# Half of a turned tile's small transfers issued on another queue, with new step tables, in a two-layer encoder trunk

## Chip, cores and metric

The kernel runs on one core of a Trainium2 chip. The metric is the device time of one execution in microseconds (us), less is better. A NeuronCore has five engines with an instruction queue each: TensorE (PE, matrix products), VectorE (DVE), ScalarE (ACT), GpSimd (POOL) and SyncE (SP, which here only issues transfers). Transfers are also issued by POOL. Whichever engine issues them, they run on the core's 16 DMA engines.

## The reference

The input x is 256 tokens by 2048 features, float32. Layer 1 is forgetting attention and a squared-ReLU MLP; layer 2 is chunked attention with a relative bias against keys and values that are projected once, and a second MLP:

```python
u = rms_norm(h, a_norm_g)
q, k, v, fz = split(u @ a_w_in)                # 16 heads of 128
h = h + forgetting_attention(...) @ a_w_out
h = h + square(relu(rms_norm(h, g) @ w1)) @ w2   # 2048 -> 8192 -> 2048
k_sh, v_sh = split(rms_norm(h, kv_norm_g) @ kv_w)
q = rms_norm(rms_norm(h, b_norm_g) @ b_w_q)
h = h + chunked_relbias_attention(q, k_sh, v_sh, b_rel) @ b_w_out
h = h + square(relu(rms_norm(h, g) @ w1)) @ w2
```

All weights are float32, about 497 MB, and each is read once from HBM.

## The kernel before

**Products.** A weight block of 128 rows and 1024 columns is loaded (`raw`), split by ACT into a rounded part `hi` (line 294) and by DVE into the rest `lo` (line 295), and multiplied in three passes, x-high by hi, x-low by hi, x-high by lo (lines 594, 596, 598). The two MLPs and layer 2's query projection save products by a Strassen-like scheme. Their weights come in pairs of blocks; for each pair seven forms (`FORMS`: "11", "T3", "T2", "T1", "21", "T4", "22") are multiplied with sums of the activations (`form_products`, line 618), and the rest of the pair's rows in plain steps "a" and "b". Some forms are sums of weight blocks: `bring` (line 309) loads a block with SP into a tile `w`, `add_on` (line 316) adds another block onto it, for T1 and T3 by an accumulating transfer that POOL issues (line 326), for T4 by DVE (line 324), and `make` (line 328) forms T2 with DVE (line 333).

**Turned tiles.** The result of a product has tokens on the partitions, but the next product needs features there. A tile of 128 partitions by 1024 elements is turned in two parts. DVE transposes its 32x32 blocks into `z` (`blocks32`, line 440, instruction on line 443); then 16 small transfers move the 32-row blocks of z to their places in `q` or `land` (`moves`, line 452, transfers on line 458). Each has 32 rows of 256 elements, 32 KB. `moves` returns four steps, of four transfers each. It is used for the new x after an output projection or an MLP (`next_x`, line 492), for the hidden activations (`turn_hidden`, line 975) and for two of layer 2's query tiles (`head_norm` with `apart`). What reads the turned tile is, for x, ACT's scaling `y` (line 419, in `split_turned`), and, for the hidden activations, ACT's ReLU in place (line 956, in `take`). Tiles elsewhere are turned through DRAM (`carry`), which the change leaves alone.

**Order.** The program text is the order of DVE, ACT, PE and SP (`keep_order`); POOL's instructions have their order from the framework that places them. Each engine works through its own queue in order. A list of fill slots runs beside the products: after each step of a plan one slot is taken off (`run_fill`, line 357), and its functions are written there. Which slot a step goes to, counted from where its tile became complete, is set by tables:

- `HIDDEN[n]`: for the n-th quarter of a hidden chunk, four move steps, then the steps of `take` (ReLU first).
- `SHORT[n]` and `LONG[n]`: for the n-th quarter of a new x after an output projection (SHORT) or an MLP's end (LONG): row sums, block transposes, four move steps, then the steps of `split_turned` (y first).
- `QUERY`, `ATT`: slots of query tiles and of the attention heads.
- `ORDER`: the steps of a pair; "f0" to "f6" are forms (two halves each), "a" and "b" plain steps, "r" a step left over from an earlier pair. An "r" is passed over when nothing is left (lines 217 to 219).
- `BEHIND[(i, s)]`: what is written some number of weight units after form i, half s, was issued: (delay, own pair or next, function, arguments).
- `OPENING`: the same ahead of a plan's first pair.

**Buffers and waits.** Weight units are issued up to three ahead of the product (`fetch`, line 348), and loaded up to four units ahead of that; `raw` has three buffers of two halves. A load that needs a buffer waits on SP until the split of the block before it is done, and what is written behind it on SP waits too.

Of the kernel before, what the change touches and what calls it, by code (L numbers as in the profile page):

```python
# [28 lines left out]
AHEAD = 2  # L29
EARLY = 4  # L30
HIDDEN = (
# [4 lines left out]
)  # L36
UA = UN // 512
LONG = (
# [4 lines left out]
)  # L43
SHORT = (
# [4 lines left out]
)  # L49
REL = 384  # L50
QUERY = (0, 1, 13, 12, 6, 17, 6)
AGAIN = (0, 1, 2, 3, 5, 5, 7, 7)
ATT = ((8, 14, 18, 18, 10), (8, 9, 12, 12, 9))
BIAS = (3, 6, 7)
ORDER = {
# [9 lines left out]
}  # L65
BEHIND = {
    (0, 0): [(0, 1, "make", 0), (4, 1, "add", "T1", 0)],
    (0, 1): [(0, 1, "make", 1)],
    (1, 1): [(3, 0, "bring", "12", 0), (3, 1, "add", "T1", 1)],
    (3, 1): [(5, 0, "bring", "11", 0), (3, 0, "bring", "11", 1)],  # L70
    (4, 0): [(0, 1, "add", "T4", 0)],
    (4, 1): [(0, 1, "add", "T4", 1), (9, 0, "add", "T3", 1)],
    (2, 1): [(3, 0, "bring", "12", 1)],
    (3, 0): [(2, 0, "add", "T3", 0)],
}
SUBS = {"1": (2, 2), "2": (2, 2), "q": (2, 2)}
OPENING = (
    (23, "bring", "12", 0),
    (17, "bring", "12", 1),
    (4, "add", "T3", 0),  # L80
    (9, "add", "T3", 1),
    (6, "bring", "11", 0),
    (1, "bring", "11", 1),
)
BIG = 2 * UN
FORMS = ("11", "T3", "T2", "T1", "21", "T4", "22")
# [14 lines left out]
def trunk(ctx: ExitStack, tc: tile.TileContext, t):  # L101
# [3 lines left out]
    V, S, G, TE, SY = nc.vector, nc.scalar, nc.gpsimd, nc.tensor, nc.sync  # L105
# [40 lines left out]
    first = sm.tile([P, GH], F32, name="first", bufs=1)  # L146
# [299 lines left out]
    def deal(at, do):  # L446
        items = [[] for _ in range(max(at) + 1)]
        for i, d in zip(at, do):
            items[i].append(d)
        add_fill(items)  # L450

    def moves(z, dst):
        n = z.shape[1] // 4
        d = dst.rearrange("p (i f) -> p i f", i=4)

        def move(i):
            for j in range(4):
                SY.dma_start(d[32 * j : 32 * j + 32, i], z[32 * i : 32 * i + 32, j * n : (j + 1) * n])  # L458

        return [lambda i=i: move(i) for i in range(4)]  # L460

# [19 lines left out]
    def landing(i):  # L481
        if not land:
            land.append(prob.tile([P, 2 * BIG], F32, name="land", tag="p", bufs=1))
        return land[0][:, i * UN : (i + 1) * UN]

    def turned(name=None):
        z = qkv.tile([P, GH * T], F32, name="z")
        return (z, qkv.tile([P, GH * T], F32, name=name, tag=name, bufs=4 if name == "s" else 2)) if name else z
# [186 lines left out]
    def head_norm(stats, z, dst, late=0, apart=None):  # L675

        rest = []

        def f(b, ps):
            sq = wk.tile([P, 512], F32, name="sq", tag="wk")  # L680
            ss = sm.tile([P, GH], F32, name="ss")
            rn = sm.tile([P, GH], F32, name="rn")

            def square():
                S.activation(sq, ps, AF.Square)

            def total():
                V.tensor_reduce(ss, sq.rearrange("p (a d) -> p a d", a=GH), axis=AX.X, op=ALU.add)

            def norm():  # L690
                vv = sm.tile([P, GH], F32, name="vv")
                V.tensor_scalar(vv, ss, 1.0 / P, stats().e[:, b : b + 1], op0=ALU.mult, op1=ALU.add)
                G.tensor_tensor(rn, vv, mhalf, op=ALU.pow)

            def turn():
                qn = wk.tile([P, 512], F32, name="qn", tag="wk")
                V.tensor_tensor(qn.rearrange("p (a d) -> p a d", a=GH), ps.rearrange("p (a d) -> p a d", a=GH),
                                rn.unsqueeze(2).to_broadcast([P, GH, P]), op=ALU.mult)
                blocks32(qn, z, b)

            if apart is None:
                square()
            rest.append((square, total, norm, turn))
            if b == NB - 1:
                turns = [[t] for _, _, _, t in rest]
                turns += carry(z, dst) if apart is None else [[m] for m in moves(z, dst)]
                if apart is not None:
                    add_fill([[]] * apart + [[s, t, n] for s, t, n, _ in rest] + turns)
                    return
                for _, total, norm, _ in rest:  # L710
                    total()
                    if not late:
                        norm()
                add_fill([[]] * (late - 1) + ([[n for _, _, n, _ in rest]] if late else []) + turns)
        return f

    def scale_q(land, layer, g):
        tag = "qs"[g // 2]
        q = qkv.tile([P, GH, T], F32, name="q", tag=tag, bufs=4 if tag == "s" else 2)
        S.activation(q.rearrange("p a (b i c) -> p (a b) i c", b=NB, i=4),  # L720
                     land.rearrange("p (i ab c) -> p ab i c", i=4, c=32), AF.Copy, scale=gqk[:, layer : layer + 1])
        return q
# [66 lines left out]
    def attend(g, q, k, v, cq, o, make_bias):  # L789
        st = [{} for _ in range(GH)]  # L790
        box = {}
        k4 = k.rearrange("p (i a b c) -> p a b i c", i=4, a=GH, b=NB)
        *at, far = ATT[g == NG - 1]
        items = [[] for _ in range(at[-1] + far + 1)]
# [16 lines left out]
    def add_fill(items):  # L811
        for i, it in enumerate(items):
            if i < len(fill):
                fill[i] = fill[i] + it
            else:
                fill.append(it)
# [210 lines left out]
    def query(g):  # L1027
        box = {}

        def f(b, ps):  # L1030
            if b == 0:
                z, lq = turned(), landing(2 + g % 2)
                box["lq"], box["f"] = lq, head_norm(lambda: st2, z, lq, apart=(*QUERY[:2], None, None)[g])
            box["f"](b, ps)
            if b == NB - 1:
                add_fill([[]] * QUERY[2 + g] + [[lambda: qs.append(scale_q(box["lq"], 1, g))]])
                if g == 1:
                    add_fill([[]] * QUERY[6] + [[st2.flip]])
                    deal(AGAIN, [again[i // 2] for i in range(8)])
# [105 lines left out]
```

## Time and profile before

| | us |
|---|---|
| median of 3 runs | 2152.24 |
| the runs | 2150.33, 2152.24, 2157.17 |
| the profiled execution's own time | 2150.54 |
| its span in the trace | 2148.8 |
| POOL busy | 168.5 |
| HBM | 239 GB/s over the span |

The profile comes from one execution. In its rows a line such as L458 is a line of the kernel; "x672" is the number of instructions, three numbers after it are the least, the middle and the largest duration in ns. A row of a timeline holds the start, the time up to the last end, the engine, the line and the operation; the square brackets behind it give how long the engine had been idle before, and what ended that. A row of the waits holds the waiting instruction, the one that released it, the total in us, the number of waits and the longest. SPq and POOLq are the queues of instructions that issue transfers or wait. "DMA q<-z" is a transfer from z to q in the chain that ended last, from its issue to its landing.

### The profile page before, as it was taken

How to read it: one execution, taken by the hardware profiler on the slowest of the kernel's cores; microseconds unless marked ns; L12 is line 12 of the kernel's file. 1: busy time of each engine (PE TensorE's matmuls, PEld its weight loads, DVE VectorE, ACT ScalarE, POOL GpSimd, SP SyncE). 2: the span in 40 equal slices, each digit the busy share in tenths (PEclk: the TensorE clock that was granted, in tenths of full speed). 3: DMA queues.
4: the chain of work that ended last, by engine and by line, in shares of the span. 5: the costliest groups of instructions: out<-in, count | busy, mean ns of one | idle time of the engine just before them, and what ended most of it. 6: DMA issues, size and time to landing. Idle time of an engine off the chain costs nothing.

```text
span 2148.8 us, 26598 instructions
## 1 busy us (share of the span) xinstructions
PE 2086.3 (97%) x9114; PEld 1697.6 (79%) x9114; DVE 1738.3 (81%) x2003; ACT 1305.8 (61%) x1567; POOL 168.5 (8%) x184
## 2 busy tenths in 40 slices
PE   9999998999999999999999999988999999999999
PEld 7888887787887887887777888877778878878877
DVE  6777775899889889888998577758898888898887
ACT  6544444667567567657676444456665675675574
POOL 1101000001001000000002000000010010000000
PEclk9999999999999999999999999999999999999999
DMA  8787786788888888889786877867788888888884
GB/s 297 238 253 234 243 249 221 246 252 257 270 265 250 254 275 252 269 260 288 223 255 201 260 230 229 266 207 247 240 261 278 263 239 259 278 253 266 265 282 156
DMA packets 166519, 538.86 MB, mean 251 GB/s; under 512 B 42848, under 2 KB 79856, under 8 KB 131568
## 3 DMA queue, kind: packets, MB, share of 16 engines
q1 hardware_dynamic: 146800, 465.86, 61.5%
q0 software_dynamic: 19584, 71.31, 18.8%
q8 instruction: 71, 1.16, 0.2%
q14 instruction: 64, 0.52, 0.1%
HBM read 497.20 MB, written 15.75 MB: 239 GB/s over the span
## 4 chain that ended last, share of the span: by engine, by line
PE 79%; DVE 8%; DMA 5%; issue 3%; SPq 3%; ACT 2%; ACTq 0%; DVEq 0%
PE acc L596 17%; PE acc L594 17%; PE acc L598 16%; PE po L598 5%; PE po L594 5%; PE po L596 5%; PE s L598 4%; PE s L594 4%; PE s L596 4%; DVE lo L295 4%; SPq L458 2%; ACT hi L294 2%; DMA q<-z 2%; DMA raw<-in_s2a 1%; DVE wT L324 1%
## 5 line engine op out<-in xcount | busy, mean ns | idle before, releaser
L295 DVE TENSOR_TENSOR lo<-raw,hi 128x1024 fp32r<-128x1024 f32 (+1 forms) x634 | 761.8, 1215 | 237.8 <-ACT hi L294 212.1
L294 ACT ACTIVATE hi<-raw 128x1024 fp32r<-128x1024 f32 (+1 forms) x634 | 661.8, 1054 | 418.8 <-PE acc L596 226.6
L594 PE MATMUL acc<-hi,act 128*128 128x512 f32 x1644 | 461.5, 396 | 23.3 <-ACT hi L294 14.5
L596 PE MATMUL acc<-hi,act 128*128 128x512 f32 x1644 | 451.4, 391 | 0.0
L598 PE MATMUL acc<-lo,act 128*128 128x512 f32 x1644 | 450.4, 390 | 0.8 <-DVE lo L295 0.8
L594 PEld LDWEIGHTS acc<-hi,act 128*128 128x128 f32 x1644 | 306.3, 188 | 94.1 <-ACT hi L294 18.1
L598 PEld LDWEIGHTS acc<-lo,act 128*128 128x128 f32 x1644 | 308.4, 188 | 68.6 <-DVE lo L295 3.8
L596 PEld LDWEIGHTS acc<-hi,act 128*128 128x128 f32 x1644 | 310.2, 189 | 66.2 <-DVE act L389 0.5
L294 ACT ACTIVATE hi<-w 128x1024 fp32r<-128x1024 f32 x204 | 214.9, 1056 | 95.0 <-PE acc L596 38.9
L295 DVE TENSOR_TENSOR lo<-w,hi 128x1024 fp32r<-128x1024 f32 x204 | 244.4, 1218 | 26.2 <-ACT hi L294 25.3
L295 DVE TENSOR_TENSOR lo<-wT,hi 128x1024 fp32r<-128x1024 f32 x136 | 163.0, 1220 | 21.7 <-ACT hi L294 21.5
L294 ACT ACTIVATE hi<-wT 128x1024 fp32r<-128x1024 f32 x136 | 142.3, 1057 | 59.8 <-PE acc L596 20.3
L594 PE MATMUL s<-hi,act 128*128 128x512 f32 x476 | 138.5, 396 | 11.4 <-ACT hi L294 11.2
L598 PE MATMUL s<-lo,act 128*128 128x512 f32 x476 | 138.0, 394 | 4.5 <-DVE lo L295 4.2
L596 PE MATMUL s<-hi,act 128*128 128x512 f32 x476 | 136.8, 392 | 0.2 <-DVE act L423 0.2
L594 PEld LDWEIGHTS s<-hi,act 128*128 128x128 f32 x476 | 89.6, 190 | 33.3 <-ACT hi L294 15.0
L598 PEld LDWEIGHTS s<-lo,act 128*128 128x128 f32 x476 | 87.8, 188 | 30.1 <-DVE lo L295 12.9
L596 PEld LDWEIGHTS s<-hi,act 128*128 128x128 f32 x476 | 90.4, 190 | 19.8 <-DVE act L423 0.6
L324 DVE TENSOR_TENSOR wT<-wT,raw 128x1024 f32<-128x1024 f32 x68 | 82.8, 1218 | 0.0
L333 DVE TENSOR_TENSOR wT<-w,w 128x1024 f32<-128x1024 f32 x68 | 82.8, 1218 | 0.0
L594 PE MATMUL po<-hi,act 128*128 128x512 f32 x272 | 72.8, 389 | 0.0
L596 PE MATMUL po<-hi,act 128*128 128x512 f32 x272 | 72.7, 389 | 0.0
(181 smaller groups left out, 2158.2 us busy)
## 6 DMA issues: line engine op xcount, KB each, us to landing
raw<-in_w_in SPq DMA_DIRECT2D x94, 512.0 KB, 5.9
raw<-in_s1a SPq DMA_DIRECT2D x32, 1024.0 KB, 6.5
raw<-in_s2a SPq DMA_DIRECT2D x32, 1024.0 KB, 7.3
raw<-in_w_kv SPq DMA_DIRECT2D x64, 512.0 KB, 5.7
raw<-in_s1b SPq DMA_DIRECT2D x32, 1024.0 KB, 6.0
raw<-in_s2b SPq DMA_DIRECT2D x32, 1024.0 KB, 7.0
q<-z SPq DMA_DIRECT2D x672, 32.0 KB, 4.5
raw<-in_w_oa SPq DMA_DIRECT2D x32, 512.0 KB, 5.7
```

Of the source, the lines that this page charges most:

```text
L294: S.activation(hi[:, c], raw[:, c], AF.Copy)
L295: V.tensor_tensor(lo[:, c], raw[:, c], hi[:, c].bitcast(F32), op=ALU.subtract)
L324: V.tensor_tensor(d, d, p.t["21", s], op=ALU.add)
L333: V.tensor_tensor(p.t["T2"][:, half(s)], p.t["T3"][:, half(s)], p.t["11"][:, half(s)], op=ALU.add)
L458: SY.dma_start(d[32 * j : 32 * j + 32, i], z[32 * i : 32 * i + 32, j * n : (j + 1) * n])
L594: TE.matmul(ps, xh, cut(hi, j), start=first, stop=False, **kw)
L596: TE.matmul(ps, xl, cut(hi, j), start=False, stop=False, **kw)
L598: TE.matmul(ps, xh, cut(lo, j), start=False, stop=last, **kw)
```

## The change

In `moves`, of the four transfers in a step the second and the fourth are issued by POOL (`G`), the first and third still by SP. Besides, the entries of the tables for slots, orders and delays are set anew. No other line differs.

```diff
--- before.py
+++ after.py
@@ -29,58 +29,56 @@
 AHEAD = 2
 EARLY = 4
 HIDDEN = (
-    (2, 2, 3, 3, 6, 8, 8, 9, 11, 11),
-    (0, 0, 2, 2, 7, 8, 8, 8, 10, 10),
-    (0, 1, 3, 3, 5, 5, 9, 9),
-    (1, 2, 2, 4, 6, 6, 9, 10),
+    (1, 3, 3, 3, 6, 8, 8, 9, 11, 11),
+    (0, 2, 2, 2, 7, 8, 8, 8, 10, 10),
+    (1, 1, 1, 5, 5, 5, 9, 9),
+    (1, 1, 3, 4, 4, 6, 8, 10),
 )
 UA = UN // 512
 LONG = (
-    (1, 0, 0, 0, 0, 1, 6, 6, 6, 9),
-    (1, 0, 0, 1, 2, 3, 6, 7, 7, 10),
-    (2, 0, 0, 0, 4, 6, 7, 7),
-    (0, 0, 1, 1, 4, 4, 8, 8),
+    (1, 0, 0, 0, 0, 0, 5, 5, 5, 5),
+    (1, 0, 0, 0, 3, 4, 6, 7, 7, 10),
+    (0, 0, 0, 0, 0, 5, 7, 7),
+    (0, 0, 1, 2, 4, 5, 8, 8),
 )
 SHORT = (
     (3, 0, 0, 0, 0, 0, 3, 3, 5, 5),
-    (8, 0, 0, 1, 2, 5, 6, 10, 14, 14),
-    (1, 0, 2, 2, 2, 3, 8, 10),
-    (0, 0, 1, 1, 1, 3, 5, 5),
+    (6, 0, 0, 1, 1, 5, 8, 9, 14, 14),
+    (0, 0, 2, 2, 3, 5, 8, 10),
+    (1, 0, 1, 1, 1, 3, 5, 5),
 )
 REL = 384
-QUERY = (0, 1, 13, 12, 6, 17, 6)
+QUERY = (0, 1, 15, 10, 5, 17, 5)
 AGAIN = (0, 1, 2, 3, 5, 5, 7, 7)
-ATT = ((8, 14, 18, 18, 10), (8, 9, 12, 12, 9))
+ATT = ((8, 14, 18, 18, 10), (8, 8, 12, 12, 9))
 BIAS = (3, 6, 7)
 ORDER = {
-    "first": "f0 r r f1 r r r f2 f3 a a r f4 f6 f5 a a b b",
-    "w10": "f0 f1 r f2 r r f4 f3 r f5 f6 a r a a a b b",
-    "w11": "f0 r f1 r f2 f4 a r f3 a a f5 a f6 b b",
-    "w20": "r f0 r r f1 f2 f4 f3 f5 a r r a b f6 b",
-    "w21": "f0 f1 f2 r f3 f4 r a f5 r r r a f6 b r",
+    "first": "f0 r r f1 r r r r f2 f3 a r a f4 r f6 f5 a a b b",
+    "w10": "f0 f1 r f2 r r f4 f3 r r f5 a f6 a a a b b",
+    "w11": "f0 r f1 r f2 f4 a r f3 r a a f5 a f6 b b",
+    "w20": "r f0 r r f1 f2 f4 f3 f5 a r r a r b f6 b",
+    "w21": "f0 f1 f2 r f3 f4 r a f5 r r f6 r b a r",
     "w20+": "r f0 r f1 f2 f4 f3 f5 a a b b f6",
-    "w21+": "f0 f1 r r f2 r r r f4 r r f5 f3 a a r f6 r a a b b",
+    "w21+": "f0 f1 r r f2 r r r r f4 r f5 f3 a a r f6 r a a b b",
     "q0": "f0 r f1 r r f2 f3 f4 a a f5 f6 b b",
-    "q1": "f0 f1 r f2 r f4 a f5 r r a r f3 b b f6",
+    "q1": "f0 f1 r f2 r f4 r a f5 r r f3 a b b f6",
 }
 BEHIND = {
-    (0, 0): [(0, 1, "make", 0), (4, 1, "add", "T1", 0)],
+    (0, 0): [(2, 1, "add", "T1", 0), (0, 1, "make", 0)],
     (0, 1): [(0, 1, "make", 1)],
-    (1, 1): [(3, 0, "bring", "12", 0), (3, 1, "add", "T1", 1)],
+    (1, 1): [(2, 0, "bring", "12", 0), (3, 1, "add", "T1", 1), (4, 0, "bring", "12", 1)],
     (3, 1): [(5, 0, "bring", "11", 0), (3, 0, "bring", "11", 1)],
-    (4, 0): [(0, 1, "add", "T4", 0)],
-    (4, 1): [(0, 1, "add", "T4", 1), (9, 0, "add", "T3", 1)],
-    (2, 1): [(3, 0, "bring", "12", 1)],
-    (3, 0): [(2, 0, "add", "T3", 0)],
+    (4, 0): [(0, 1, "add", "T4", 0), (1, 0, "add", "T3", 0)],
+    (4, 1): [(0, 1, "add", "T4", 1), (8, 0, "add", "T3", 1)],
 }
 SUBS = {"1": (2, 2), "2": (2, 2), "q": (2, 2)}
 OPENING = (
     (23, "bring", "12", 0),
-    (17, "bring", "12", 1),
-    (4, "add", "T3", 0),
+    (19, "bring", "12", 1),
+    (6, "add", "T3", 0),
     (9, "add", "T3", 1),
-    (6, "bring", "11", 0),
-    (1, "bring", "11", 1),
+    (3, "bring", "11", 0),
+    (4, "bring", "11", 1),
 )
 BIG = 2 * UN
 FORMS = ("11", "T3", "T2", "T1", "21", "T4", "22")
@@ -455,7 +453,7 @@
 
         def move(i):
             for j in range(4):
-                SY.dma_start(d[32 * j : 32 * j + 32, i], z[32 * i : 32 * i + 32, j * n : (j + 1) * n])
+                (SY, G)[j % 2].dma_start(d[32 * j : 32 * j + 32, i], z[32 * i : 32 * i + 32, j * n : (j + 1) * n])
 
         return [lambda i=i: move(i) for i in range(4)]
```

## The prediction

> **What bounds the kernel now.** The page comes first: what is busy, and what the chain that ended last is made of.
>
> ```profile
> span 2148.8 us, 26598 instructions
> ...
> PE 2086.3 (97%) x9114; PEld 1697.6 (79%) x9114; DVE 1738.3 (81%) x2003; ACT 1305.8 (61%) x1567; POOL 168.5 (8%) x184
> ...
> PE 79%; DVE 8%; DMA 5%; issue 3%; SPq 3%; ACT 2%; ACTq 0%; DVEq 0%
> ```
>
> TensorE is the bound. All its idle time is 2148.8 - 2086.3 = 62.5 us, with start and tail in it, so a change to the transfers can win some tens of us at most. POOL is nearly idle; an issuing instruction on SP isn't counted as busy, so SP has to be read elsewhere. The second view is the timeline of PE, for the waits that it shows in brackets.
>
> ```profile
> 356.25 1.21 PE L594 MATMUL acc<-hi,act 128*128 128x512 f32 x4 [2.28 <-ACT hi L294]
> 371.89 2.07 PE L594 MATMUL acc<-hi,act 128*128 128x512 f32 x4 [4.24 <-ACT hi L294]
> ...
> 423.20 2.08 PE L594 MATMUL s<-hi,act 128*128 128x512 f32 x4 [3.87 <-ACT hi L294]
> ...
> 650.55 0.73 PE L594 MATMUL s<-hi,act 128*128 128x512 f32 x2 [1.11 <-ACT hi L294]
> ...
> 1057.50 0.73 PE L594 MATMUL acc<-hi,Sh 128*128 128x512 f32 x2 [1.75 <-ACT hi L294]
> 1075.23 0.73 PE L598 MATMUL s<-lo,act 128*128 128x512 f32 x2 [1.79 <-DVE lo L295]
> ...
> 1427.65 1.21 PE L594 MATMUL acc<-hi,act 128*128 128x512 f32 x4 [2.90 <-ACT hi L294]
> 1442.67 1.54 PE L594 MATMUL acc<-hi,act 128*128 128x512 f32 x4 [3.62 <-ACT hi L294]
> ...
> 1495.01 2.08 PE L594 MATMUL s<-hi,act 128*128 128x512 f32 x4 [4.68 <-ACT hi L294]
> ```
>
> Six of these (356, 372, 423 and the same places of the second layer, 1428, 1443, 1495) hold 2.28 + 4.24 + 3.87 + 2.90 + 3.62 + 4.68 = 21.6 us. The third view, the waits of all engines, says why ACT was late there.
>
> ```profile
> POOL w L326 <- DVE wT L333: 594.1, 35, 66.5
> ...
> POOL w L326 <- DMA w<-in_f1b: 47.8, 4, 16.1
> ...
> ACT y L419 <- DMA q<-z: 32.6, 6, 7.2
> ...
> ACT q L956 <- DMA q<-z: 10.3, 11, 2.3
> ```
>
> The turned tile's small transfers (q<-z, line 458) hold ACT six times, 32.6 us in all, in front of y (line 419), and eleven times in front of the squared ReLU (line 956). ACT is in order, so the next weight split (hi, line 294) stands behind the waiting y. This is the time that the change works on. After a long wait PE also starts slowly:
>
> ```profile
> 371.89 2.07 PE acc L594 x4
> 373.97 1.45 PE acc L596 x4
> ```
>
> ```profile
> 458.42 0.91 PE acc L594 x4
> ```
>
> Four dense matmuls take 0.91, so the wait at 372 costs 2.07 + 1.45 - 1.82 = 1.7 us more. The last row also gives the length of a plain step of the plan: twelve matmuls, 3 x 0.91 = 2.7 us; a half of a form step is 1.4.
>
> **What a transfer costs on either queue.** The views of the two lines (minimum/median/maximum in ns), the landing times, and SP's timeline:
>
> ```profile
> L458 SPq DMA_DIRECT2D q<-z x672: 507/589/1992, 340.9 to 2078.9; - x168
> L458 SPq DMA_DIRECT2D land<-z x64: 507/589/1631, 1074.1 to 1170.3; - x64
> ...
> DMA to landing us min/median/max: 1.8/4.4/9.5
> ```
>
> ```profile
> L326 POOL DMA_DIRECT2D w<-in_f1a x32: 854/867/1228, 312.1 to 940.3; - x32
> ...
> DMA to landing us min/median/max: 5.3/6.1/11.2
> ```
>
> ```profile
> 340.90 10.12 SPq L458 DMA_DIRECT2D q<-z  x16
> ...
> 357.90 2.41 SPq L458 DMA_DIRECT2D q<-z  x4
> 360.35 1.54 SPq L279 DMA_DIRECT2D raw<-in_w_oa  x3
> 361.93 2.47 SPq L458 DMA_DIRECT2D q<-z  x4
> ...
> 405.10 7.49 SPq L458 DMA_DIRECT2D q<-z  x12
> 412.69 0.53 SPq L281 DMA_DIRECT2D raw<-in_s1a  x1
> 413.27 2.41 SPq L458 DMA_DIRECT2D q<-z  x4
> ```
>
> ```profile
> 350.43 1.87 DMA q<-z
> ...
> 363.81 6.08 DMA q<-z
> ...
> 415.08 4.26 DMA q<-z
> ```
>
> There are 672 + 64 = 736 such transfers, 16 for each of 46 tiles, at 10.12 / 16 = 0.63 us a piece on SP. The change gives 368 of them to POOL. Nothing of before shows a 32-row transfer on POOL. The nearest row is the accumulating load of line 326, 128 rows of 4 KB, at 0.867. If POOL pays by rows, 32 rows cost 0.22; the slowest of that row cost 1.23. I take 0.867: the row is nearly constant (854 at least, 867 in the middle), which looks like a price for each instruction. The landing after a POOL issue lies between 1.87 (the same bytes from SP) and 5.3 (the least of a sixteen times larger one); I take 2.2, near the same bytes, with the 0.28 that POOL's issue is longer. Both ends stay in the range. POOL's busy time would rise by 368 x 0.867 = 319 us, to about 490 of 2149, which by itself hides beside PE.
>
> **The change, place by place.**
>
> First tile of the output projection's stage (340.9). Sixteen issues stand back to back, the last one starts at 350.4 and lands 1.87 later, at 352.3; y starts then. With two queues SP's half starts its last issue at 340.9 + 7 x 0.63 = 345.3, POOL's at 340.9 + 7 x 0.867 = 347.0, which lands at 349.2: 3.1 us earlier. The ends: with 0.22 on POOL, SP's half is last, 347.2, 5.1 earlier; with 1.23 and a landing of 5.3 it is 354.8, 2.5 later. PE waits 2.28 here and 2.90 in the second layer, so 3.1 removes both: **5.2**.
>
> Second tile (371.9). Its moves stand between weight loads, and a load's issue waits until DVE has freed a buffer. From 357.9 on SP issues 8 moves; 4 fewer are 4 x 0.63 = 2.5. The new SHORT[1] also puts the first y from slot 6 to slot 8, 2 x 2.7 = 5.5 us later in ACT's order, so splits pass ahead of it. Together that is more than ACT's longest wait, 7.2. PE's 4.24 + 3.62 and the slow restart (1.7 and 1.54 - 0.91 = 0.6) could go: 10.2. But y is then late for the products that read it, and half of SP's moves still land behind loads in the same queue (6.08). I take half: **5**.
>
> Third place (423.2). Twelve moves, a load, four moves. If the load's buffer comes free no earlier, only two of the last four issues go, 2 x 0.63 = 1.3 a layer: **2.6**. If it does, 6 more come off. PE's waits of 3.87 and 4.68 are the ceiling.
>
> MLP stages. 32 of the 46 tiles are hidden ones. Their moves bring PE to a stop seldom: 1.11 at 650, and 1.75 and 1.79 around 1057 to 1075, where loads stand behind moves on SP. I take **2.2** of the 4.65 (about half, as SP loses half of the issues).
>
> Tables of order. An "r" of ORDER with nothing left over does nothing (lines 217 to 219). Counting the leftovers from pair to pair, the new "first", "w11", "w20" and "w21+" give the very same order as the old ones. Only "w21" (f6 ahead of the last a), "w10" (the fifth r ahead of f5 and f6) and "q1" (f3 ahead of the a) differ, by a step or two, with the same products: 0.
>
> Adds on POOL (lines 316 to 326). They now share their queue with moves. An add behind 8 moves starts up to 8 x 0.867 = 6.9 us later; and moves behind an add wait for what it waits for, as below. New waits for splits of w: I take a **loss of 3** against that, between 0 (they hide, POOL's adds mostly wait long for make of line 333) and the 12 of the rival below.
>
> Sum: 5.2 + 5 + 2.6 + 2.2 - 3 = 12.0 us less. The profiled execution itself took 2150.54, 1.7 above its span; the median of the three runs is 2152.24, and the forecast is given against that: 2152.24 - 12 = **2140**.
>
> The Trainium skill, "DMA: Bandwidth & Descriptors", section "Issuing engines are not separate DMA queues", says that issuing from several engines saves only the sequencer's time for starting a transfer, usually small beside the transfer. Here the row speaks differently on size: 10.12 us of issue against 1.87 of landing. By the page's rule that the issue time alone is saved, the first place gives the same figure as mine, but the second and third would give no shorter landing, which I did not count either.
>
> **The rivals.**
>
> A. *The moves wait behind an add on POOL* (slower). POOL is in order. The add onto the brought "12" waits for that load:
>
> ```profile
> 486.92 0.33 SPq L313 DMA_DIRECT2D w<-in_f2a  x1
> ```
>
> ```profile
> 492.50 1.75 POOL L326 DMA_DIRECT2D w<-in_f2a  x2 [7.60 <-DMA w<-in_f2a]
> ```
>
> The load is issued at 486.9 and the adds start at 492.5, 5.6 us later, as soon as it lands. A move behind them starts 5.6 + 1.75 = 7.3 us late. It decides where the tile is turned inside that stretch, and more than about 3 us (the time that halving saves) before its end. The new BEHIND has the load one unit earlier, but the first add much closer behind it: in the second pair only three half steps, 4.1 us, less than 5.6. Against it: POOL reaches most adds far ahead (594.1 us of waiting for make). If one tile in three of 46, 15, loses 7.3 - 3 = 4.3 us, and PE feels 1.6 of each (as the 1.1 to 1.8 above), that is +24, and with the gain of 12: 2152 + 12 = **2164**.
>
> B. *Another engine takes the time back* (no change). DVE is 81% busy over the span; where ACT stops waiting, the lo split may come last, as at 1075. Or POOL's half is as late as the whole was: the first place breaks even where 7p + landing = 11.4, with a landing of 2.2 at p = 1.31, of 5.3 at p = 0.87. Then the change does not do what it says: **2151**.
>
> C. *All six waits go.* 21.6 with some 6 of slow restarts and no loss on POOL: **2124**.
>
> D. *DVE starves POOL* (slower). The slowest row of POOL's loads, 1.23, would then be the usual one, and each move slower still beside dense DVE work: at p = 1.6, 7 x 1.6 + 2.2 = 13.4 against 11.4 now, 2 us later at six places, +12: **2164**. Against it: 81% of DVE beside loads at 854 to 867. The Trainium skill, "SBUF — State Buffer", section "SBUF: two separate sides", the box on DVE blocking DMA, states that a DVE operation in a two-port mode locks POOL out while it writes descriptors, 620 ns becoming 3100; the steady rows of line 326 don't agree for this kernel's mix.
>
> **How the numbers follow.** A measurement of this kernel can tell about 0.3%, 6.5 us. Forecast (2128 to 2146): 0.50. C: 0.08. B, within 0.3%: 0.17. A: 0.20, D: 0.05. Faster 0.50 + 0.08 = 0.58, same 0.17, slower 0.25. The range goes from C's 2124, less 2 for POOL issues at 0.22, to A's 2164 with 2 for a late landing: 2122 to 2166. The forecast's own range is 2128 to 2146.
>
> **What would show it.** Line 458 on POOL, 368 times, at 0.8 to 0.9 us each, and POOL near 490 us busy. ACT's wait for q<-z at y down from 32.6 to below 15. PE's gaps at 356 and 1428 gone, at 372 and 1443 halved. If A holds, moves on POOL start right behind adds that waited for a load of w, and ACT at line 956 waits more than 10.3. It is wrong if POOL's issues take over 1.3 us, if the six gaps stand as they are, or if new gaps of 1 to 2 us come up in the MLP stages.

## The result, and the profile after

The changed kernel takes **2116.68 us** (median of 4 runs, 2115.48 to 2120.32), the kernel before 2154.70 on the same chip (4 runs, 2150.33 to 2157.32). The ratio is 0.9828, with an interval of 0.9805 to 0.9852: faster by 38 us. The forecast was 2140, its range 2122 to 2166, so the time lies below the range. The sign was right and the size was a third of what came.

The page of the changed kernel, the lines that answer to those of before. All of its line numbers lie 2 lower: L456 is the move, L324 the add, L292 and L293 the splits, L417 y, L954 the ReLU, L592 to L596 the matmuls.

```profile
span 2113.7 us, 27078 instructions
...
PE 2074.7 (98%) x9114; PEld 1695.1 (80%) x9114; DVE 1736.8 (82%) x2003; ACT 1301.9 (62%) x1567; POOL 354.1 (17%) x552
...
PE 83%; DMA 6%; DVE 6%; issue 3%; ACT 2%; SPq 0%; POOL 0%; ACTq 0%; DVEq 0%; POOLq 0%
```

The span of the profiled executions fell by 2148.8 - 2113.7 = 35.1 us. In the chain that ended last, SP's queue went from 3% to 0%. PE's own busy time fell too, by 11.6 us, with the same 9114 matmuls: more of them ran at the full granted clock (the share of full speed that the profile shows for PE). POOL rose by 185.6 us for 368 moves, half a microsecond each, where the forecast had 319 us.

Where the time came from is read from the busy time by stretches, before and after, cut at the same points of the program: the first output projection's stage, the first MLP with the query projection, the second output projection's stage. Columns: stretch, its length, busy time and count of PE, PEld, DVE, ACT, POOL, then granted clock of PE, DMA share, GB/s. Before:

```profile
334.80:453.00 118.20, 106.05 (x447) 85.37 (x447) 88.04 (x98) 71.34 (x96) 6.95 (x8) 0.97 0.73 229
453.00:1171.00 718.00, 697.22 (x3017) 561.98 (x3018) 633.12 (x648) 481.50 (x530) 64.71 (x69) 1.00 0.83 256
1405.60:1525.00 119.40, 106.32 (x448) 85.52 (x448) 88.23 (x98) 71.38 (x95) 6.87 (x8) 0.97 0.73 226
```

After:

```profile
334.70:439.20 104.50, 102.42 (x447) 83.51 (x447) 88.35 (x98) 71.43 (x95) 29.90 (x54) 1.00 0.83 257
439.20:1155.00 715.80, 696.96 (x3019) 565.21 (x3020) 632.45 (x647) 478.20 (x529) 146.66 (x231) 1.00 0.84 257
1387.70:1492.50 104.80, 102.41 (x448) 83.52 (x448) 88.22 (x98) 71.60 (x95) 28.83 (x52) 1.00 0.85 261
```

The two output projection stages give 13.7 + 14.6 = **28.3 us**, four fifths of the whole. The MLP with the query projection gives 2.2. The rest, from stretches not shown, is 1.9 in layer 2's attention (234.6 to 232.7), 2.6 in the second MLP (623.8 to 621.2) and 0.1 at the start. In the two stages PE's busy time falls by 3.63 + 3.91 = 7.5 us with equal counts of matmuls, and the granted clock goes from 0.97 to 1.00: those are the slow restarts that went with the waits.

The waits on turned tiles, from the waits of the changed kernel:

```profile
ACT q L954 <- DMA q<-z: 23.9, 7, 5.2
```

```profile
ACT y L417 <- DMA q<-z: 1.8, 2, 1.2
```

ACT's wait at y, 32.6 us before, is 1.8: the six places are gone. Its wait at the ReLU has grown from 10.3 to 23.9, which none of the forecast's steps has; the runs with the slots of hidden tiles below follow it up. One wait of PE grew as well, on its timeline near the end of the MLP with the query projection:

```profile
1073.68 1.19 PE L592 MATMUL po<-hi,S 128*128 128x512 f32 x2 [3.90 <-DVE s L637]
```

It is 4.21 with the queue alone, and it was 1.72 before:

```profile
1088.88 0.70 PE L594 MATMUL po<-hi,S 128*128 128x512 f32 x2 [1.72 <-DVE s L639]
```

The traces show where it comes from. In the changed kernel, POOL's timeline ahead of it, and ACT's:

```profile
1056.00 0.92 POOL L324 DMA_DIRECT2D w<-in_fqb  x1 [20.64 <-DVE wT L331]
1057.19 1.51 POOL L456 DMA_DIRECT2D land<-z  x3 [0.27 <-issue]
1059.30 1.47 POOL L456 DMA_DIRECT2D land<-z  x3 [0.60 <-issue]
1060.76 0.97 POOL L324 DMA_DIRECT2D w<-in_fqb  x1
```

```profile
1070.61 1.06 ACT L292 ACTIVATE hi<-w 128x1024 fp32r<-128x1024 f32 x1 [3.37 <-DMA w<-in_fqb]
```

The second add stands behind six moves in POOL's queue, and ACT's split of its sum waits 3.37 us until it has landed; before, ACT's longest wait for an add was 1.2. DVE's half of that split stands ahead of the tile s that PE waits for. So an add that comes late among the moves, which the forecast had among its losses, does come up here, and PE's wait is 3.90 - 1.72 = 2.2 us longer.

The two timelines that answer to SP's of before, first SP's, from the first tile on:

```profile
340.76 5.03 SPq L456 DMA_DIRECT2D q<-z  x8
345.88 0.53 SPq L277 DMA_DIRECT2D raw<-in_w_oa  x1
346.51 1.14 SPq L456 DMA_DIRECT2D q<-z  x2
347.70 0.57 SPq L277 DMA_DIRECT2D raw<-in_w_oa  x1
348.32 3.31 SPq L456 DMA_DIRECT2D q<-z  x4
351.73 2.24 SPq L277 DMA_DIRECT2D raw<-in_w_oa  x4
354.01 1.15 SPq L456 DMA_DIRECT2D q<-z  x2
```

POOL's at the same place, and the first y on ACT's:

```profile
341.02 7.88 POOL L456 DMA_DIRECT2D q<-z  x16 [27.87 <-DVE z L441]
```

```profile
347.66 1.71 ACT L417 ACTIVATE y<-q,gsb 128x256 f32<-128x256 f32 x4 [0.57 <-DMA q<-z]
```

POOL issues its eight moves of the first tile and its eight of the second in one run, 7.88 / 16 = 0.49 each. Nothing on POOL holds the second tile back, while SP has its weight loads between. The first y starts at 347.66; it was 352.45 before, and 349.2 by the forecast. The view of the moves' line on POOL, with the landing of all moves:

```profile
L456 POOL DMA_DIRECT2D q<-z x336: 496/498/1184, 341.0 to 2033.8; - x168
...
DMA to landing us min/median/max: 1.7/5.9/13.1
```

A move costs POOL 0.498 in the middle, SP 0.589 as before. The landing has become longer, from 4.4 to 5.9. So what is won is time of issue; the transfers themselves don't arrive sooner after it.

### The profile page after: what moved, and what is told of

The parts are those of the page before. It is cut to its first block, busy times and chain, and to the rows that moved or that the text cites. A ratio compares the mean times of both kernels' runs of the same rounds, so it can differ in the third digit from the quotient of the medians.

```text
span 2113.7 us, 27078 instructions
## 1 busy us (share of the span) xinstructions
PE 2074.7 (98%) x9114; PEld 1695.1 (80%) x9114; DVE 1736.8 (82%) x2003; ACT 1301.9 (62%) x1567; POOL 354.1 (17%) x552
## 4 chain that ended last, share of the span: by engine, by line
PE 83%; DMA 6%; DVE 6%; issue 3%; ACT 2%; SPq 0%; POOL 0%; ACTq 0%; DVEq 0%; POOLq 0%
PE acc L592 18%; PE acc L594 18%; PE acc L596 18%; PE po L592 5%; PE po L596 5%; PE po L594 5%; PE s L596 4%; PE s L592 4%; PE s L594 4%; DVE lo L293 3%; DMA raw<-in_s2a 2%; DMA q<-z 2%; ACT hi L292 2%; DVE wT L322 1%; DMA raw<-in_s2b 1%
## 5 line engine op out<-in xcount | busy, mean ns | idle before, releaser
L293 DVE TENSOR_TENSOR lo<-raw,hi 128x1024 fp32r<-128x1024 f32 (+1 forms) x634 | 759.5, 1214 | 221.2 <-ACT hi L292 208.9
L292 ACT ACTIVATE hi<-raw 128x1024 fp32r<-128x1024 f32 (+1 forms) x634 | 660.4, 1054 | 386.7 <-PE acc L594 224.5
L592 PE MATMUL acc<-hi,act 128*128 128x512 f32 x1644 | 459.0, 394 | 9.9 <-DVE acc L637 4.4
L596 PE MATMUL acc<-lo,act 128*128 128x512 f32 x1644 | 449.1, 390 | 0.3 <-DVE lo L293 0.3
L592 PEld LDWEIGHTS acc<-hi,act 128*128 128x128 f32 x1644 | 306.1, 188 | 79.5 <-DVE acc L637 7.9
L596 PEld LDWEIGHTS acc<-lo,act 128*128 128x128 f32 x1644 | 307.5, 188 | 66.8 <-DVE lo L293 2.4
L292 ACT ACTIVATE hi<-w 128x1024 fp32r<-128x1024 f32 x204 | 215.1, 1056 | 100.6 <-PE acc L594 39.6
L293 DVE TENSOR_TENSOR lo<-w,hi 128x1024 fp32r<-128x1024 f32 x204 | 244.5, 1216 | 27.9 <-ACT hi L292 27.2
L456 POOL DMA_DIRECT2D q<-z x336 | 174.1, 608 | 464.1 <-DVE z L441 253.8
L292 ACT ACTIVATE hi<-wT 128x1024 fp32r<-128x1024 f32 x136 | 142.4, 1057 | 65.7 <-PE acc L594 27.0
L293 DVE TENSOR_TENSOR lo<-wT,hi 128x1024 fp32r<-128x1024 f32 x136 | 162.7, 1218 | 21.9 <-ACT hi L292 21.8
L596 PE MATMUL s<-lo,act 128*128 128x512 f32 x476 | 137.7, 394 | 2.6 <-DVE lo L293 2.4
L592 PE MATMUL s<-hi,act 128*128 128x512 f32 x476 | 136.4, 391 | 0.8 <-ACT hi L292 0.8
L596 PEld LDWEIGHTS s<-lo,act 128*128 128x128 f32 x476 | 87.9, 188 | 27.0 <-DVE lo L293 9.7
L592 PEld LDWEIGHTS s<-hi,act 128*128 128x128 f32 x476 | 89.4, 188 | 20.6 <-ACT hi L292 2.0
L691 POOL TENSOR_TENSOR rn<-vv,mhalf 128x4 f32<-128x4 f32 x32 | 44.3, 1398 | 336.4 <-DVE vv L690 336.3
```

Of the source, the lines that this page charges most:

```text
L292: S.activation(hi[:, c], raw[:, c], AF.Copy)
L293: V.tensor_tensor(lo[:, c], raw[:, c], hi[:, c].bitcast(F32), op=ALU.subtract)
L456: (SY, G)[j % 2].dma_start(d[32 * j : 32 * j + 32, i], z[32 * i : 32 * i + 32, j * n : (j + 1) * n])
L592: TE.matmul(ps, xh, cut(hi, j), start=first, stop=False, **kw)
L596: TE.matmul(ps, xh, cut(lo, j), start=False, stop=last, **kw)
```

## The experiments

**The queue and the tables apart.** First the one line of `moves` alone, on the kernel before:

```diff
-                SY.dma_start(d[32 * j : 32 * j + 32, i], ...)
+                (SY, G)[j % 2].dma_start(d[32 * j : 32 * j + 32, i], ...)
```

> The kernel before with one line changed: every second small transfer on POOL; all tables as before. Theory 1 (the queue does it: a tile's transfers end sooner because SP issues half of them, and the tables only follow): most of the gain of 35 us, 20 to 35 us less than before, with ACT's waits for q<-z in front of y under 10 us instead of 32.6. Theory 2 (the tables do it: y moved later in ACT's order is what frees ACT): at most 10 us less, and the waits at the second tile (7.18 and 6.55) stand within 2 us.

Measured: **2108.84 us** (2108.65 to 2111.33; before 2152.89), ratio 0.9794 [0.9768, 0.9820]. The queue alone gives all of the gain and, by the medians, some 8 us more than the whole change; the intervals of the two ratios just overlap. Its two stages take 104.4 and 105.6 us, as in the changed kernel. The forecast let the second tile's wait go by two things together, fewer moves on SP and a later slot of y (SHORT[1], 6 to 8). Here y keeps its old slot. ACT's timeline at the second tile:

```profile
361.13 0.91 ACT L419 ACTIVATE y<-q,gsb 128x256 f32<-128x256 f32 x2 [3.17 <-DMA q<-z]
```

ACT still waits 3.17, but no wait of PE over 1 us is left there: the new slot isn't needed.

Then the tables alone: the changed kernel with all moves back on SP.

```diff
-                (SY, G)[j % 2].dma_start(d[32 * j : 32 * j + 32, i], ...)
+                SY.dma_start(d[32 * j : 32 * j + 32, i], ...)
```

> The changed kernel with all small transfers back on SP; tables as changed. Theory 1: 0 to 12 us less than before, or slower, since some new slots leave less room behind the last move. Theory 2: 20 to 35 us less than before. If the two parts simply add, this run and the queue alone sum to 35 us.

Measured: 2209.86 us (2207.33 to 2212.63), ratio 1.0258 [1.0224, 1.0292]. With one queue the new tables cost 57 us. The waits and PE's timeline of this kernel:

```profile
ACT q L954 <- DMA q<-z: 49.0, 18, 5.7
```

```profile
672.82 1.22 PE L592 MATMUL po<-hi,Sh 128*128 128x512 f32 x2 [4.79 <-ACT hi L292]
```

The waits at hidden tiles go from 10.3 to 49.0 us, and PE stops for them in the MLP, at 672.82. The parts don't add up: the queue alone -44, the tables alone +57, both -38. The new tables place their steps for moves that are ready sooner than one queue can issue them.

**Which table.** The changed kernel with HIDDEN as it was, all else of the change kept:

```diff
-    (1, 3, 3, 3, 6, 8, 8, 9, 11, 11),
-    (0, 2, 2, 2, 7, 8, 8, 8, 10, 10),
-    (1, 1, 1, 5, 5, 5, 9, 9),
-    (1, 1, 3, 4, 4, 6, 8, 10),
+    (2, 2, 3, 3, 6, 8, 8, 9, 11, 11),
+    (0, 0, 2, 2, 7, 8, 8, 8, 10, 10),
+    (0, 1, 3, 3, 5, 5, 9, 9),
+    (1, 2, 2, 4, 6, 6, 9, 10),
```

> The changed kernel with the table HIDDEN of before; everything else as changed. The theory that HIDDEN is what the new tables lose (its third and fourth rows put the last move into the slot of the ReLU, or the ReLU two slots earlier) expects the time of the queue alone, 2107 to 2112 us, and ACT's waits for q<-z at line 954 down from 23.9 to under 5 us. The rival that it is BEHIND with its earlier loads and adds expects 2114 to 2119, as the changed kernel.

Measured: 2111.82 us (2108.45 to 2113.51; before 2154.49), ratio 0.9795 [0.9776, 0.9815]. That is the queue alone again: the tables of order, delays and the other slots together come to nothing that can be measured. With the old HIDDEN ACT's wait at the ReLU is gone:

```profile
ACT q L954 <- DMA q<-z: 1.9, 2, 1.0
```

The counterpart, the queue with the new HIDDEN and nothing else (the same rows set the other way, on the kernel before with its one line):

> The queue alone (tables of before), with the new HIDDEN. The theory that HIDDEN holds what the new tables lose expects the time of the changed kernel, 2114 to 2120 us, with ACT's waits for q<-z at line 956 over 15 us. If it stays at 2107 to 2111, the loss is in the other tables or in their sum.

Measured: 2115.58 us (2111.55 to 2120.37; before 2158.71), ratio 0.9801 [0.9773, 0.9828]:

```profile
ACT q L956 <- DMA q<-z: 22.7, 8, 5.7
```

The wait at the ReLU follows HIDDEN in all four kernels: 23.9 and 22.7 with the new rows, 1.9 in the old ones above and 1.9 again with the queue alone. In the new third and fourth rows the ReLU stands in the slot of the last move (5 and 5, 4 and 4), in the old ones two slots behind it (3 and 5, 4 and 6). So the wait is shown to be HIDDEN's. What it does to the time is less sure: 5 to 8 us by medians, 1 to 7 by the ratios to the kernel before on the same chip (0.9828 and 0.9801 against 0.9794 and 0.9795). The intervals of the ratios overlap, so a loss of time by HIDDEN is likely, and not shown.

**How many moves on POOL.** All of them, with the new tables and with the old ones, and one in four:

```diff
-                (SY, G)[j % 2].dma_start(d[32 * j : 32 * j + 32, i], ...)
+                G.dma_start(d[32 * j : 32 * j + 32, i], ...)
```

> The changed kernel with all 16 small transfers of a tile on POOL, none on SP. If only the number of issues in a row counts (16 x 0.50 = 8.0 us on POOL against 10.1 on SP before and 5.0 now), it lies between: 8 to 20 us less than before. If what counts is that moves stand behind weight loads that wait for a buffer on SP, or hold loads up there, it is about as fast as the changed kernel, within 8 us of it.

Measured: 2196.26 us (2187.14 to 2204.57), ratio 1.0196 [1.0156, 1.0237], slower than both expectations; ACT's wait at the ReLU is 74.5 us there.

> The kernel before with all small transfers on POOL, tables of before. The theory that one queue for all 16 moves is the trouble, whichever it is, expects no gain to speak of: 2135 to 2165 us, with POOL waiting many times for its own q<-z. The theory that it is the company of weight loads on SP expects 2105 to 2120.

Measured, the same line on the kernel before: 2162.43 us (2160.14 to 2168.57), ratio 1.0037 [1.0024, 1.0051]. One of its waits, and POOL's timeline at the first tile:

```profile
POOL q L458 <- DMA q<-z: 87.0, 92, 3.1
```

```profile
341.13 3.99 POOL L458 DMA_DIRECT2D q<-z  x8 [26.92 <-DVE z L443]
345.80 3.90 POOL L458 DMA_DIRECT2D q<-z  x8 [0.68 <-DMA q<-z]
```

A free queue with the cheaper issue is worth nothing by itself: with all sixteen moves on it, POOL also waits 92 times for an earlier transfer of its own, 87 us in all. The two rows show how: eight issues follow each other, and the ninth starts only when the first has landed. In no trace of these runs does POOL have more than eight transfers on the way. ACT waits for tiles longer than before, 27.0 us at y and 34.6 at the ReLU, against 32.6 and 10.3.

```diff
-                SY.dma_start(d[32 * j : 32 * j + 32, i], ...)
+                (SY, SY, SY, G)[j].dma_start(d[32 * j : 32 * j + 32, i], ...)
```

> The kernel before with one small transfer in four on POOL, three on SP; tables of before. SP then issues 12 x 0.63 = 7.6 us for a tile instead of 10.1. If the time follows the longer of the two halves, it takes half of the gain of the queue alone: 2125 to 2135 us. If it is enough that SP's last moves come a little earlier, 2108 to 2118.

Measured: 2132.05 us (2130.07 to 2133.41), ratio 0.9876 [0.9857, 0.9894]. With the old tables the series of ratios is 1 (none on POOL), 0.9876 (a quarter), 0.9794 (half), 1.0037 (all). A quarter less on SP gives some 27 of the 44 us, and PE still waits 3.66 us at the second tile, where it waited 4.24 before.

**Another engine as the second queue.** ACT in POOL's place, on the kernel before:

```diff
-                SY.dma_start(d[32 * j : 32 * j + 32, i], ...)
+                (SY, S)[j % 2].dma_start(d[32 * j : 32 * j + 32, i], ...)
```

> The queue alone, with ScalarE's queue in place of POOL's: every second move issued by ACT. The theory that any second queue helps expects 2105 to 2125 us. The theory that it must be an idle engine expects a loss: ACT is in order and 61% busy, so each move on it holds up the weight splits behind it, by the wait for z and by the issue (0.5 us x 368 = 184 us): above 2160.

Measured: 2219.20 us (2217.91 to 2221.18), ratio 1.0296 [1.0278, 1.0315]. SP has the same half to issue as with POOL, and yet the time rises by some 64 us. One of its waits:

```profile
ACT hi L294 <- DMA q<-z: 57.2, 18, 9.3
```

ACT's issue costs about what SP's does (0.602 us in the middle, 0.588 on SP), but ACT's splits of weights now stand behind moves in its queue. So POOL is the right engine because what stands behind its moves is seldom pressed, and not only because there is a second queue.

**Rival A: moves behind adds.** The text's order for POOL as well, which the framework otherwise sets; nothing else differs from the changed kernel:

```diff
-    keep_order(tc, (V.engine, S.engine, TE.engine, SY.engine))
+    keep_order(tc, (V.engine, S.engine, TE.engine, SY.engine, G.engine))
```

> The changed kernel with POOL's instructions too held to the order of the program text (one more engine in the call at line 1077). As it is, the framework puts up to 16 moves behind one add or a pair of adds. Rival A of the prediction (moves late behind adds that wait) expects a change of 5 us or more either way, with ACT's waits for q<-z at line 954 moving from 23.9 to under 10 us if the written order is better. The theory that moves behind adds cost nothing expects the same time within 3 us.

Measured: 2149.81 us (2145.01 to 2162.95, 10 runs), ratio 0.9990 [0.9970, 1.0009]: the gain is gone, 33 us over the changed kernel. The profile is of the slowest of the ten runs. POOL's timeline:

```profile
657.02 0.86 POOL L324 DMA_DIRECT2D w<-in_f2a  x1 [8.77 <-DMA w<-in_f2a]
657.82 3.54 POOL L456 DMA_DIRECT2D q<-z  x7
...
666.20 0.50 POOL L456 DMA_DIRECT2D q<-z  x1 [4.84 <-DMA w<-in_f2a]
```

Seven moves start right behind an add that had waited 8.77 us for its load. The eighth waits 4.84 us more, until that add's own transfer has landed: it is the eighth transfer behind it. Soon after, at 673.56, PE waits 4.10 us for a weight split. This is rival A as the forecast described it, at a price of 33 us where the forecast had 24. What the run tests is the order as a whole: adds behind moves are in it too. In the changed kernel, too, POOL's moves wait for adds' transfers (14 times, 27.6 us), but ACT's wait at y is 1.8 us there and 9.6 in this run, and PE has no wait over 1.2 us that ends with a weight split by ACT.

**What POOL's price decides.** Three runs make POOL's half later, all on the kernel with the queue alone. First each of POOL's moves in two halves of 128 columns, so that POOL has sixteen issues a tile:

```diff
-                (SY, G)[j % 2].dma_start(d[32 * j : 32 * j + 32, i], z[32 * i : 32 * i + 32, j * n : (j + 1) * n])
+                if j % 2:
+                    for k in (slice(0, n // 2), slice(n // 2, n)):
+                        G.dma_start(d[32 * j : 32 * j + 32, i, k], z[32 * i : 32 * i + 32, j * n : (j + 1) * n][:, k])
+                else:
+                    SY.dma_start(d[32 * j : 32 * j + 32, i], z[32 * i : 32 * i + 32, j * n : (j + 1) * n])
```

> The queue alone, with each of POOL's small transfers cut into two of 32 x 128 elements: POOL issues 16 x 0.50 = 8.0 us for a tile instead of 4.0, SP 8 moves as in the queue alone, with no operation of POOL's added that could meet DVE. This is near the price that the prediction took (8 x 0.867 = 6.9). If the price of POOL's issue was the term that the prediction had too high, most of the gain goes: 2140 to 2165 us. If the price hardly counts and the copies of the two runs before did the harm in another way, it stays at 2107 to 2118.

Measured: 2156.47 us (2154.16 to 2161.10, 10 runs; before 2153.84), ratio 1.0016 [1.0005, 1.0028]. One more issue of 0.5 us for each move of POOL takes back the whole gain. PE's timeline in the first stage:

```profile
356.46 2.08 PE L598 MATMUL acc<-hi,act 128*128 128x512 f32 x4 [3.05 <-ACT hi L294]
...
417.73 2.08 PE L598 MATMUL s<-hi,act 128*128 128x512 f32 x4 [3.06 <-ACT hi L294]
```

The waits at the first tile and at the third place are back; at the second tile PE doesn't wait over 1 us. So the first and third places hang on how long POOL's half takes, the second on SP's queue. Half of a tile takes POOL 16 x 0.498 = 8.0 us here and 4.0 with eight issues. A straight line between the two times, which is assumed, gives 2109 + (6.9 - 4.0) / 4.0 x 47.6 = 2143 us at the forecast's 6.9 (8 x 0.867). But the price isn't the only thing that changes. POOL waits for transfers of its own 76 times, 71.4 us, much as with all moves on it. And the first stage takes 113.1 us, still less than the 118.2 of before, while the first MLP with the query projection takes some 732, more than its 718.0; PE's longest wait there, 7.64 us at 1096.77, comes behind a split that waits 7.10 for an add behind halved moves. So the run bounds the effect of the price from above.

Second, a copy of 32 rows by POOL ahead of each of its moves, to the places that the move then overwrites; no work is left out:

```diff
+                if j % 2:
+                    G.tensor_copy(d[32 * j : 32 * j + 32, i], z[32 * j : 32 * j + 32, :n])
```

> The queue alone (tables of before), and ahead of each small transfer on POOL a copy of 32 x 256 elements on POOL that reads z and writes the place that the transfer then fills; so POOL's price for a move goes from 0.50 to some 0.8 to 1.0 us, near the 0.867 of the prediction. The theory that the prediction failed by this price expects most of the difference to the forecast: 2125 to 2145 us. The rival, that POOL's half has room (it starts ahead of SP's, which stands among weight loads), expects 2107 to 2115.

Measured: 2195.22 us (2191.76 to 2195.49), ratio 1.0181 [1.0162, 1.0200]. POOL's timeline shows 0.95 us for a move with its copy, near the forecast's price:

```profile
340.85 0.85 POOL L459 COPY q<-z 32x256 f32<-32x256 f32 x2 [26.84 <-DVE z L443]
341.64 1.06 POOL L460 DMA_DIRECT2D q<-z  x2
```

It is slower than with the halved moves, though eight of these steps take 7.6 us a tile and not 8.0, and the page of this run shows why it can't be read as a price alone. DVE does the same 2003 instructions in 1780.8 us, against 1735.4 with the queue alone: the copies slow it down.

Third, three copies of one column each ahead of each move of POOL, again to places that the move overwrites:

```diff
+                for k in range(3 * (j % 2)):
+                    G.tensor_copy(d[32 * j : 32 * j + 32, i, k : k + 1], z[32 * j : 32 * j + 32, k : k + 1])
```

> The queue alone, and ahead of the transfers on POOL three copies of 32 x 1 elements for each (written to a place that the transfer then fills): POOL's time for a tile grows, while DVE is hardly touched, unlike with the long copies, where DVE's busy time rose from 1735 to 1781 us. If the longer copies cost 86 us because POOL's half came later, this run costs by the same measure: in proportion to POOL's added time, 2120 us or more for 0.3 us on each transfer. If they cost it through DVE, it stays at 2107 to 2115.

Measured: 2282.38 us (2280.01 to 2284.10), ratio 1.0572 [1.0551, 1.0592]. POOL's timeline:

```profile
341.54 6.84 POOL L459 COPY q<-z 32x1 f32<-32x1 f32 x24 [27.21 <-DVE z L443]
348.33 3.99 POOL L460 DMA_DIRECT2D q<-z  x8
```

The 24 copies stand ahead of the eight moves and take 6.84 us at the first tile; DVE's busy time stays (1740.8). So here, too, a late half on POOL costs without coming through DVE, some 123 us over the time before: rival B's mechanism is real and could have gone well past no change. The price isn't held at one value, though, and POOL's adds stand behind the copies as well, so the run doesn't tell how the time goes between 4.0 and 6.9.

## Why the prediction was too small

**First tile: right, 5.2 of 5.2.** The wait of 2.28 and that of layer 2 are gone. y came 4.8 us earlier, where 3.1 were counted, and by the other path of the forecast. It had POOL's half last. The issues of this tile in the changed kernel, POOL's eight and the first seven of SP's, with the median time to landing:

```profile
q<-z POOLq DMA_DIRECT2D x8, 32.0 KB, 1.8
q<-z SPq DMA_DIRECT2D x7, 32.0 KB, 1.9
```

The eighth issue on POOL starts at 341.02 + 7 x 0.49 = 344.5 and is there by 346.3, while SP's eighth starts at 340.76 + 7 x 0.63 = 345.2 and lands at about 347.1. So SP's half is last, as the forecast had it for its low end of 5.1. The price of 0.867 was the mis-sized term (0.49 measured), with a landing of 1.8 where 2.2 was taken.

**Second tile: the first step that failed.** The prediction said: "From 357.9 on SP issues 8 moves; 4 fewer are 4 x 0.63 = 2.5", and from that "I take half: **5**". It counted only the moves behind the last load that it looked at, on the ground that a load holds the queue until DVE frees a buffer. The rows of before between those that were quoted show that nothing held it. SP's timeline before:

```profile
351.12 0.53 SPq L279 DMA_DIRECT2D raw<-in_w_oa  x1
351.75 2.41 SPq L458 DMA_DIRECT2D q<-z  x4
354.20 0.58 SPq L279 DMA_DIRECT2D raw<-in_w_oa  x1
354.82 2.40 SPq L458 DMA_DIRECT2D q<-z  x4
357.33 0.53 SPq L279 DMA_DIRECT2D raw<-in_w_oa  x1
```

Each row starts where the one above ends. From 340.90 to 364.40 SP issued without a pause, 32 moves among six loads. Sixteen moves less, of 0.63 each, are 10.1 us. In the changed kernel SP's last move of that tile ends at 354.01 + 1.15 = 355.2; from the first move on that is 14.4 us against 23.5, so 9.1 came off and not 2.5. The whole 10.2 of waits and restarts went. That it went with the old slot of y is shown by the queue alone, and that it hangs on SP and not on POOL's price is shown by the halved moves.

**Third place: the second.** "If the load's buffer comes free no earlier, only two of the last four issues go": 2.6. The other case, which the prediction named, held. SP's timeline of the changed kernel at this place:

```profile
396.15 3.69 SPq L456 DMA_DIRECT2D q<-z  x6
399.94 0.52 SPq L279 DMA_DIRECT2D raw<-in_s1a  x1
400.50 1.15 SPq L456 DMA_DIRECT2D q<-z  x2
```

The load goes after six moves, and from the first move to the end of the last it is 5.5 us, where it was 10.6 (405.10 to 415.68). The 3.87 and 4.68 went, 8.55 in all, but for 0.3 and 0.5.

**Slow restarts.** The forecast had them at the second tile alone, 1.7 + 0.6. Four of the six waits had them. Twelve matmuls take 2.72 us when dense. Behind the wait of 3.62 they take 4.46 (1442.67 to 1447.13), so 1.7 more and not 0.6, and at the third place 4.22 in both layers (423.20 to 427.42, 1495.01 to 1499.23). Behind the first tile's 2.28 and 2.90 the granted clock stays at 1.00. PE's busy time in the two stages fell by 7.5 us in all. With this the stages' working closes: 5.2 + 10.2 + 8.55 + (7.5 - 2.3) = 29.1 against 28.3 measured and 12.8 forecast.

**Elsewhere.** The MLPs, the query projection and the attention gave 6.8 against 2.2 less a loss of 3. The loss is of the right kind and about the right size: PE waits 2.2 us more behind the add among the moves. So it is the gain of 2.2 that was too small; where the rest of it comes from, the 1.9 in the attention too, wasn't traced. Order tables at 0: nothing speaks against it, as all tables but HIDDEN together come to nothing measurable. Slots of hidden tiles were counted at nothing without a reason; ACT waits 21 to 22 us more at the ReLU by the new HIDDEN, and the time that this costs isn't settled.

**Rivals and range.** C was the true case, with all six waits, 21.6 and 6 of restarts (7.5). It stopped at 2124 because it took nothing outside of the two stages: 2152.24 - 27.6 - 6.8 = 2117.8. A and B are mechanisms that the runs showed in other kernels (+33 by the order; no gain left with the halved moves), so weight on them wasn't idle, but the change meets their conditions at few places. D, moves of 1.6 us on POOL, falls: 0.498 in the middle, 1.184 at most.

**The Trainium skill**, "DMA: Bandwidth & Descriptors", section "Issuing engines are not separate DMA queues", says that several issuers save only the sequencer's time. That is borne out, as the landings didn't get shorter (4.4 to 5.9). It calls this time usually small beside the transfer. Of a single move that holds (0.63 to issue, 4.4 to land), but sixteen in a row take 10.12 us where the last one lands 1.87 later, and issuing half of them elsewhere is worth 44 us of 2153 with the queue alone.

**The fastest version by medians** is the old tables with the one line of `moves`: 2108.84 us, ratio 0.9794 [0.9768, 0.9820] to the kernel before, then the new tables but for HIDDEN with 2111.82. Both are below the changed kernel's 2116.68, with intervals that overlap.

## What to carry to other kernels

Before counting what a shorter queue brings, read its rows end to end: where each issue starts as the last one ends, the queue is the limit over that whole stretch, and everything taken out of it counts, not only what stands behind the last load. Where a case that removes all waits of one kind is among the rivals, add to it the restarts at each wait and what the other stages would give, since it sets the end of the range. And a second queue pays on the engine whose next work isn't pressed, and only while its half stays short: 4 us of issue for half of a tile gave 2%; 8 us, with twice the transfers, gave nothing.

## What the runs showed of the hardware

- A plain transfer of 32 rows costs POOL 0.498 us to issue, less than SP (0.589) and ACT (0.602), and not the 0.867 of its accumulating one with 128 rows; 16 KB pieces of 128 columns cost it 0.498 as well, so it isn't the bytes.
- Behind PE's waits of 3.62 to 4.68 us its granted clock is 0.55 to 0.60 over the next 3.4 us; behind the waits of 2.28 and 2.90 it is 1.00. In the kernel before, behind the wait at 372, nine matmuls run in 3.4 us at 0.55, and behind the one at 356 fifteen at 1.00:

```profile
371.90:375.30 3.40, 3.40 (x9) 2.70 (x10) 3.40 (x4) 3.40 (x7) 0.00 (x0) 0.55 0.58 184
356.25:359.65 3.40, 3.40 (x15) 2.78 (x16) 3.37 (x6) 0.94 (x2) 0.00 (x0) 1.00 0.70 213
```

- POOL's copies slow DVE. With a 32x256 copy ahead of each POOL move, DVE's largest group, lo from raw and hi, takes 1240 ns in the mean, where it is 1214 with the queue alone. The copies themselves take 387 ns at least and 856 in the middle; that DVE is what slows them is likely, and wasn't shown. Copies of a single column take 182 in the middle and up to 1264, with hardly a cost to DVE's sum (1740.8 against 1735.4).
- POOL waits for its own transfers when it issues many, in no trace with more than eight on the way: 92 times with sixteen a tile, four times with eight (queue alone, 6.3 us).
